# Attention operand loads taken one by one over five tiles, start-up transfers reordered, and pair weights asked for at tick 5

## The chip, the core and the metric

The kernel runs on one core of one Trainium2 chip. The metric is the device time of one execution in microseconds (us). A core has five instruction streams: TensorE (PE, matrix products), VectorE (DVE), ScalarE (ACT), GpSimd (POOL) and SyncE (SP), which here does nothing but issue transfers between DRAM and on-chip memory (DMAs). Each stream runs its instructions in the order in which they were written, and an instruction that must wait holds up everything behind it on the same stream, DMA issues included.

## The reference

One decoder block, on x of 1024 tokens by 1024 channels, all float32:

```
h = rms_norm(x);  z = h @ w_in                    # q, k, v, glu_in, two gates
attention: 3 groups (dilation 1, 4, 16) x 8 heads of 64, window 128 keys,
           relative bias; p = softmax(q k^T / 8 + bias); o = p v
           the 3 groups' outputs are merged by their softmax denominators, @ w_attn_out
conv:      GLU, causal depthwise convolution of 31 taps, layer norm, silu, @ w_conv_out
x = x + rms_norm((sigmoid(z_ga) * attn + sigmoid(z_gc) * conv) @ w_mix_out)
x = x + rms_norm(swiglu(rms_norm(x)))             # hidden width 2816
```

## The kernel before

**Arithmetic.** Every operand of a large product is split into a high part (rounded) and a low part (the rest), and three matmuls of high and low parts make one product. ACT makes the high part, DVE or POOL subtracts it to get the low part. Most products are done in a seven-product block scheme (`winograd`, L320, called for pairs of weight tiles).

**Stages, in PE's order.** `start` (L479) computes the first projections while it loads x and three weight tiles. Then come GLU and gate projections and the query and key projections (`qk_pair`, L778), all by pairs of weight tiles (`pair`, L270), with the convolution on DVE beside them. Then `v` (L891) computes the values, and attention runs beside it: `beat` (L133) steps the generator `attention` (L932) after each matmul at a fixed rate. Attention goes on beside the convolution's output projection (L1444 ff.). Then the mixing projection, the FFN and its output follow.

**Attention.** There are 96 tiles: 12 pairs of heads with 8 query blocks (u = 0 to 7) each. For one tile PE computes scores (`att_s`, L980: matmuls at L995; DVE adds the bias tile and takes the minimum at L998), ACT takes the exponential (`att_e`, L1008), three tiles later PE transposes (`att_t`, L1031) and ACT and DVE split the result (L1036, L1037), and four tiles later PE multiplies with the values (`att_p`, L1052 and L1054) and DVE adds the parts (L1059). The outputs go to DRAM by stores at L1017 and L1021 (`datt`), statistics to `dst`.

**Loads of the next pair.** Queries and keys were stored in DRAM (`dq`, `dk`). `stacks` (L833) issues all loads of one pair of heads: per head a half tile of queries twice (L841, L842, 256 KB each) and the keys (L843, 512 KB), and then the bias tile (L474, 256 KB, from `rep`). `attention` calls it when u has reached 2 (L968). `double` (L849, POOL) copies the queries to the other half of their tiles when u reaches 6 and 7. `values` (L868) loads the next values (`dv`) as soon as the last were split (`value_parts`, L882: ACT L887, POOL L888).

**What sets the order.** Nothing reorders instructions: the order of each stream is that of the program text as it is executed when the kernel is built. `tick` (L115) counts matmul steps and runs steps planned for a tick. `pair` plans the splits of the current weights and the load of the next two tiles (`load_ahead`, L171) at tick `LD` after the pair's start. On-chip tiles come from a pool of 44 buffers of 512 KB (`slot`) and one of 13 buffers of 256 KB (`half`). A new tile takes a released buffer, and the first instruction that writes it waits for the last one that used the buffer, which may be a store that still reads it. SP's DMAs leave in program order, and each waits, besides, for the DMA that was issued eight before it.

Of the kernel before, what the change touches and what calls it, by code (L numbers as in the profile page):

```python
# [10 lines left out]
F32R = mybir.dt.float32r  # L11
# [7 lines left out]
H = 512  # L19
# [13 lines left out]
RV, RU = 0.42, 0.8  # L33


LD, PC = 7, (18, 20, 26)

FIRST = 4

# [17 lines left out]
def f(ap):  # L57
    return ap.bitcast(F32)


class Build:
# [417 lines left out]
    def start(self, jobs):  # L479


        nc = self.nc
        n = len(jobs)
        xs = [self.slot() for _ in range(KT)]
        for i in jobs:
            self.raw[i] = self.slot()
        self.sent = self.queued = jobs[-1] + 1
        for hf in range(2):
            nc.sync.dma_start(xs[0][:, hf * H:(hf + 1) * H], self.xT[0][:, hf * H:(hf + 1) * H])
        self.consts()  # L490
        for i in jobs:
            nc.scalar.dma_start(self.raw[i][:, :256], self.jobs[i][0][:, :256])
        nc.sync.dma_start(xs[1], self.xT[1])
        for i in jobs:
            nc.sync.dma_start(self.raw[i][:, 256:], self.jobs[i][0][:, 256:])
        for kt in range(2, KT):
            nc.sync.dma_start(xs[kt], self.xT[kt])
        self.par = self.small.tile([128, NPAR], F32, name="par")
        nc.gpsimd.dma_start(self.par, self.p_par)
        banks = [[self.bank() for _ in range(2)] for _ in range(n)]  # L500
        W = [(self.slot(F32R), self.slot(F32R)) for _ in range(n)]
        self.hH, self.hL, acc = [], [], None

        def weight_parts(i, kt):
            s = slice(kt * 128, (kt + 2) * 128)
            wh, wl = W[i]
            nc.scalar.copy(wh[:, s], self.raw[jobs[i]][:, s])
            nc.vector.tensor_tensor(wl[:, s], self.raw[jobs[i]][:, s], f(wh[:, s]), op=OP.subtract)

        def square(kt):  # L510
            q = self.slot()
            nc.scalar.activation(q, xs[kt], AF.Square)
            if acc is not None:
                nc.vector.tensor_tensor(q, q, acc, op=OP.add)
            return q

        weight_parts(0, 0)
        for kt in range(KT):
            hi, lo = self.slot(F32R), self.slot(F32R)
            for s in (slice(0, H), slice(H, T)) if kt == 0 else (slice(0, T),):  # L520
                nc.scalar.activation(hi[:, s], xs[kt][:, s], AF.Copy, scale=self.gains[:, kt:kt + 1])
                nc.vector.scalar_tensor_tensor(lo[:, s], xs[kt][:, s], self.gains[:, kt:kt + 1], f(hi[:, s]),
                                               op0=OP.mult, op1=OP.subtract)
            if kt % 2 == 0:
                for i in range(n):
                    if kt or i:
                        weight_parts(i, kt)

            if kt:
                acc = square(kt - 1)  # L530
            self.hH.append(hi)
            self.hL.append(lo)
        acc = square(KT - 1)
        for i in jobs:
            del self.raw[i]
        self.load_ahead(jobs[-1] + 2)
        self.queue_split(jobs[-1] + 2)
        norm = self.rstd(acc, T, self.eps_rms)
        pb = None
        for kt in range(KT):  # L540
            s = slice(kt * 128, (kt + 1) * 128)
            for i in range(n):
                for a, b in ((W[i][0], self.hH), (W[i][0], self.hL), (W[i][1], self.hH)):
                    for hf in range(2):
                        nc.tensor.matmul(banks[i][hf], a[:, s], b[kt][:, hf * H:(hf + 1) * H],  # L545
                                         start=kt == 0 and a is W[i][0] and b is self.hH,
                                         stop=kt == KT - 1 and a is W[i][1])
                self.tick()
            if kt == KT - 3:
                next(norm)  # L550
            if kt == KT - 2:
                try:
                    next(norm)
                except StopIteration as e:
                    pb = e.value
        self.rs = self.slot()
        for hf in range(2):
            nc.scalar.copy(self.rs[:, hf * H:(hf + 1) * H], pb[hf])
        self.xs = xs
        return banks  # L560
# [270 lines left out]


    def stacks(self, g, hp):  # L833

        nc = self.nc
        dk, dq = self.d_qk[g, hp]
        ops = []
        top, low = slice(0, 64), slice(64, 128)
        for h in range(2):
            k, a, b = self.slot(F32R), self.slot(F32R), self.slot(F32R)  # L840
            nc.sync.dma_start(f(a[top]), dq[h][top])  # L841
            nc.sync.dma_start(f(b[low]), dq[h][low])  # L842
            nc.sync.dma_start(f(k), dk[h])  # L843
            ops.append((k, a, b))
        bt = self.bias_tile(g, hp)
        st = self.tiny(96, "stat", 3).rearrange("p (g u e) -> p g u e", g=3, u=8)
        return [g, hp, ops, bt, st]

    def double(self, p, hf):  # L849

# [81 lines left out]
    def attention(self):  # L932

        live, s, total = {}, 0, 96
        order = [(g, 2 * hg + i) for hg in range(2) for g in range(3) for i in range(2)]
        nxt, cur, u, x, V = self.stacks(*order.pop(0)), None, 8, None, None

        def there():
            return nxt[1] // 2 * 3 + nxt[0] < self.vn

        while s < total + self.LP:
            if s < total:
                if x is None and nxt and there():
                    x = self.values(*nxt[:2])
                if u == 8:
                    while not self.normed or x is None:
                        if x is None and there():
                            x = self.values(*nxt[:2])
                        yield 0
                    if cur is None:  # L950
                        self.double(nxt, 0)
                        self.double(nxt, 1)
                    V, cur, u, nxt = [], nxt, 0, None
                live[s] = a = {}
                self.att_s(a, cur, V, u)
                u += 1

                if u in (3, 4):
                    V.append(self.value_parts(x, u - 3))
                    if u == 4:  # L960
                        x = None
                if u == 6 and cur[0] == 2:
                    self.other_stats(cur)
                if u in (6, 7) and nxt:
                    self.double(nxt, u - 6)
                if u == 8:
                    cur[2] = cur[3] = V = None
                if u == 2 and order:  # L968
                    nxt = self.stacks(*order.pop(0))
            if 0 <= s - 1 < total:  # L970
                self.att_e(live[s - 1])
            yield 0
            if 0 <= s - self.LT < total:
                self.att_t(live[s - self.LT])
                yield 0
            if 0 <= s - self.LP < total:
                yield from self.att_p(live.pop(s - self.LP))
            s += 1
# [929 lines left out]
```

## Time and profile before

| what | value |
|---|---|
| time, median of 3 runs (lowest to highest) | 1756.43 us (1753.7 to 1757.82) |
| time of the profiled execution | 1755.95 us |
| span in its trace, first to last instruction | 1754.2 us |
| PE busy | 1713.3 us, 98% of the span |
| DVE, ACT, POOL busy | 1244.9, 794.3, 459.6 us |
| moved by DMA | 277.03 MB, 158 GB/s over the span |
| granted PE clock, mean | 0.992 |

A row of the waits says who waited for whom, the total in us, how many times, and the longest. A row of the timeline has start, duration, engine, line and operation, and in brackets the idle time of the engine just before and what ended it; SPq and ACTq are DMA issues. A row of the windows gives for each engine the busy time in that stretch, then the granted PE clock (1.00 is full), the busy share of the DMA engines and the GB/s moved.

### The profile page before, as it was taken

What the parts mean: (1) busy time and instruction counts of PE and PEld (TensorE: products, weight loads), DVE (VectorE), ACT (ScalarE), POOL (GpSimd) and SP (SyncE); (2) the same over time, 40 slices, a digit from 0 to 9 for tenths busy, and PEclk for the clock granted to TensorE, in tenths of its full rate; (3) what the DMA queues carried; (4) which work ended last, traced back from release to release, by engine and by line L of the source; (5) the groups of instructions that cost most, each with busy time, mean ns of one, the idle gap of its engine ahead of it and who ended that gap; (6) DMA issues with size and microseconds to landing.
All of it is one profiled execution on the core that took longest, in us unless ns stands there. A gap on an engine that the chain in (4) does not pass through costs nothing.

```text
span 1754.2 us, 24483 instructions
## 1 busy us (share of the span) xinstructions
PE 1713.3 (98%) x8698; PEld 1456.1 (83%) x8698; DVE 1244.9 (71%) x2217; ACT 794.3 (45%) x1552; POOL 459.6 (26%) x337
## 2 busy tenths in 40 slices
PE   8999999999999999998899999999999999999998
PEld 6778888887788999998788888888888888888886
DVE  6879988898997666685575665585665655667686
ACT  6344444343344476666543245643333333354453
POOL 0017778787785133342300130000000000000000
PEclk9999999999999999998899999999999999999999
DMA  4342333466678797886755742212232232395234
GB/s 161 122 159 96 124 135 126 151 193 171 165 168 195 234 274 205 226 228 161 202 191 181 279 164 87 96 72 90 91 133 101 91 109 107 132 341 180 96 126 152
DMA packets 186406, 277.03 MB, mean 158 GB/s; under 512 B 56321, under 2 KB 108028, under 8 KB 186284
## 3 DMA queue, kind: packets, MB, share of 16 engines
q1 hardware_dynamic: 185596, 274.84, 49.9%
q8 instruction: 68, 1.11, 0.3%
q14 instruction: 54, 0.44, 0.1%
q10 hardware_dynamic: 576, 0.40, 0.1%
q0 software_dynamic: 112, 0.24, 0.0%
HBM read 184.81 MB, written 95.33 MB: 160 GB/s over the span
## 4 chain that ended last, share of the span: by engine, by line
PE 88%; DMA 3%; ACT 3%; DVE 2%; issue 2%; POOL 1%; SPq 0%; DVEq 0%; ACTq 0%; POOLq 0%
PE p L315 14%; PE p L317 14%; PE p L316 14%; PE p L1792 12%; PE p L303 5%; PE p L299 5%; PE p L301 5%; PE p L1521 5%; PE p L913 2%; PE p L911 2%; PE p L915 2%; PE p L545 2%; PE p L995 2%; PE p L1031 1%; PE p L1054 1%
## 5 line engine op out<-in xcount | busy, mean ns | idle before, releaser
L315 PE MATMUL p<-b,b 128*128 128x512 f32 x1204 | 469.7, 390 | 4.5 <-DVE c L820 2.7
L317 PE MATMUL p<-b,b 128*128 128x512 f32 x1204 | 469.1, 390 | 0.3 <-POOL b L190 0.3
L316 PE MATMUL p<-b,b 128*128 128x512 f32 x1204 | 468.9, 389 | 0.0
L315 PEld LDWEIGHTS p<-b,b 128*128 128x128 f32 x1204 | 226.4, 188 | 53.5 <-DVE c L820 4.1
L317 PEld LDWEIGHTS p<-b,b 128*128 128x128 f32 x1204 | 226.2, 188 | 48.0 <-POOL b L190 1.0
L316 PEld LDWEIGHTS p<-b,b 128*128 128x128 f32 x1204 | 226.4, 188 | 47.3
L189 ACT CAST b<-b 128x1024 fp32r<-128x1024 f32 x131 | 137.8, 1052 | 173.0 <-POOL b L210 65.7
L1792 PE MATMUL p<-b,b 128*128 128x512 f32 x924 | 209.6, 389 | 0.0
L1792 PEld LDWEIGHTS p<-b,b 128*128 128x128 f32 x924 | 173.4, 188 | 36.0
L190 POOL TENSOR_TENSOR b<-b,b 128x1024 fp32r<-128x1024 f32 x66 | 158.9, 2408 | 127.5 <-ACT b L189 109.9
L190 DVE TENSOR_TENSOR b<-b,b 128x1024 fp32r<-128x1024 f32 x65 | 79.5, 1223 | 127.6 <-ACT b L189 127.6
L675 DVE SCALAR_TENSOR_TENSOR p<-b,par,p 128x511 f32<-128x511 f32 (+14 forms) x232 | 163.4, 738 | 0.0
L299 PE MATMUL p<-b,b 128*128 128x512 f32 x368 | 147.9, 402 | 0.0
L303 PE MATMUL p<-b,b 128*128 128x512 f32 x368 | 147.0, 399 | 0.0
L301 PE MATMUL p<-b,b 128*128 128x512 f32 x368 | 146.6, 398 | 0.0
L913 PE MATMUL p<-b,b 128*128 128x256 f32 x384 | 115.7, 301 | 1.5 <-DVE b L183 1.5
L911 PE MATMUL p<-b,b 128*128 128x256 f32 x384 | 115.9, 302 | 0.6 <-ACT b L182 0.6
L915 PE MATMUL p<-b,b 128*128 128x256 f32 x384 | 114.9, 299 | 0.0
L1137 DVE TENSOR_TENSOR b<-b,b 128x512 fp32r<-128x512 f32 x117 | 80.6, 692 | 24.1 <-ACT b L1136 22.4
L1137 DVE TENSOR_TENSOR b<-c,b 128x512 fp32r<-128x512 f32 x101 | 70.1, 694 | 38.1 <-ACT b L1136 37.6
L1136 ACT CAST b<-b 128x512 fp32r<-128x512 f32 x117 | 72.4, 620 | 50.6 <-DVE b L1649 12.6
L1037 DVE TENSOR_TENSOR c<-p,c 128x256 fp32r<-128x256 f32 (+1 forms) x96 | 52.3, 545 | 54.1 <-ACT c L1036 51.8
(224 smaller groups left out, 3020.3 us busy)
## 6 DMA issues: line engine op xcount, KB each, us to landing
b<-w_in SPq DMA_DIRECT2D x53, 512.0 KB, 5.1
b<-w_fi SPq DMA_DIRECT2D x44, 512.0 KB, 5.0
dk<-c SPq DMA_DIRECT2D x96, 128.0 KB, 3.0
dq<-c SPq DMA_DIRECT2D x96, 128.0 KB, 2.4
b<-dq SPq DMA_DIRECT2D x48, 256.0 KB, 7.7
b<-dk SPq DMA_DIRECT2D x24, 512.0 KB, 8.0
dqS<-c SPq DMA_DIRECT2D x44, 256.0 KB, 2.1
b<-w_fo SPq DMA_DIRECT2D x44, 256.0 KB, 4.6
```

Of the source, the lines that this page charges most:

```text
L190: self.wsplit.tensor_tensor(lo, x, f(hi), op=OP.subtract)
L299: nc.tensor.matmul(ps, hi[:, s], a, start=kt == 0, stop=False)
L301: nc.tensor.matmul(ps, hi[:, s], b, start=False, stop=False)
L303: nc.tensor.matmul(ps, lo[:, s], a, start=False, stop=kt == nk - 1)
L315: nc.tensor.matmul(ps, hi[:, s], a, start=first and kt == 0, stop=False, skip_group_check=True)
L316: nc.tensor.matmul(ps, hi[:, s], b, start=False, stop=False, skip_group_check=True)
L317: nc.tensor.matmul(ps, lo[:, s], a, start=False, stop=kt == 3, skip_group_check=True)
L675: nc.vector.scalar_tensor_tensor(A[i][:, j:], src[i][:, :H - j], w[i], A[i][:, j:], op0=OP.mult, op1=OP.add)
L911: nc.tensor.matmul(o, a, hi[:, s], start=kt == 0, stop=False)
L913: nc.tensor.matmul(o, a, lo[:, s], start=False, stop=False)
L1137: nc.vector.tensor_tensor(s[:, 512:512 + n], src, f(s[:, :n]), op=OP.subtract)
L1792: nc.tensor.matmul(acc[t], x, y, start=first and e == 0, stop=last and e == 2, skip_group_check=True)
```

## The change

1. `LD` goes from 7 to 5: the next pair's weights are asked for two ticks sooner.
2. In `start`, the first transfers leave in another order. The left half of the first x tile goes out on ACT's queue ahead of the gains; SP begins with the first quarter of the first weight tile, then the right half of that x tile, the first quarters of the other two weight tiles, the second x tile, the rest of the weights, the rest of x. Before, SP began with both halves of x, and ACT issued the three weight quarters behind the gains.
3. `stacks` only makes the record of the next pair, now when u has reached 1. A new function, `stack_load`, loads one part in each of five tiles: the queries of the first head (u = 1), of the second head (u = 2), the keys of the first (u = 3), of the second (u = 4), the bias tile (u = 5).

```diff
-LD, PC = 7, (18, 20, 26)
+LD, PC = 5, (18, 20, 26)
...
-        for hf in range(2):
-            nc.sync.dma_start(xs[0][:, hf * H:(hf + 1) * H], self.xT[0][:, hf * H:(hf + 1) * H])
+        nc.scalar.dma_start(xs[0][:, :H], self.xT[0][:, :H])
+        w = [(self.raw[i], self.jobs[i][0]) for i in jobs]
+        nc.sync.dma_start(w[0][0][:, :256], w[0][1][:, :256])
+        nc.sync.dma_start(xs[0][:, H:], self.xT[0][:, H:])
         self.consts()
-        for i in jobs:
-            nc.scalar.dma_start(self.raw[i][:, :256], self.jobs[i][0][:, :256])
+        for x, d in w[1:]:
+            nc.sync.dma_start(x[:, :256], d[:, :256])
         nc.sync.dma_start(xs[1], self.xT[1])
-        for i in jobs:
-            nc.sync.dma_start(self.raw[i][:, 256:], self.jobs[i][0][:, 256:])
+        for x, d in w:
+            nc.sync.dma_start(x[:, 256:], d[:, 256:])
...
     def stacks(self, g, hp):
+        st = self.tiny(96, "stat", 3).rearrange("p (g u e) -> p g u e", g=3, u=8)
+        return [g, hp, [[None] * 3, [None] * 3], None, st]
+
+    def stack_load(self, p, i):
...
+        if i < 2:
+            a, b = self.slot(F32R), self.slot(F32R)
+            nc.sync.dma_start(f(a[top]), dq[i][top])
+            nc.sync.dma_start(f(b[low]), dq[i][low])
+            p[2][i][1:] = a, b
+        elif i < 4:
+            k = self.slot(F32R)
+            nc.sync.dma_start(f(k), dk[i - 2])
+            p[2][i - 2][0] = k
+        else:
+            p[3] = self.bias_tile(p[0], p[1])
...
         nxt, cur, u, x, V = self.stacks(*order.pop(0)), None, 8, None, None
+        for i in range(5):
+            self.stack_load(nxt, i)
...
-                if u == 2 and order:
+                if u == 1 and order:
                     nxt = self.stacks(*order.pop(0))
+                if u < 6 and nxt:
+                    self.stack_load(nxt, u - 1)
```

More of the change, by code (lines that the diff above doesn't have):

```diff
@@ L487, in start @@
         self.sent = self.queued = jobs[-1] + 1
-        for hf in range(2):
-            nc.sync.dma_start(xs[0][:, hf * H:(hf + 1) * H], self.xT[0][:, hf * H:(hf + 1) * H])
+        nc.scalar.dma_start(xs[0][:, :H], self.xT[0][:, :H])
+        w = [(self.raw[i], self.jobs[i][0]) for i in jobs]
+        nc.sync.dma_start(w[0][0][:, :256], w[0][1][:, :256])
+        nc.sync.dma_start(xs[0][:, H:], self.xT[0][:, H:])
         self.consts()
-        for i in jobs:
-            nc.scalar.dma_start(self.raw[i][:, :256], self.jobs[i][0][:, :256])
+        for x, d in w[1:]:
+            nc.sync.dma_start(x[:, :256], d[:, :256])
         nc.sync.dma_start(xs[1], self.xT[1])
-        for i in jobs:
-            nc.sync.dma_start(self.raw[i][:, 256:], self.jobs[i][0][:, 256:])
+        for x, d in w:
+            nc.sync.dma_start(x[:, 256:], d[:, 256:])
+        w = x = None
         for kt in range(2, KT):
@@ L833, in stacks @@
     def stacks(self, g, hp):
+        st = self.tiny(96, "stat", 3).rearrange("p (g u e) -> p g u e", g=3, u=8)
+        return [g, hp, [[None] * 3, [None] * 3], None, st]
+    def stack_load(self, p, i):
         nc = self.nc
-        dk, dq = self.d_qk[g, hp]
-        ops = []
+        dk, dq = self.d_qk[p[0], p[1]]
         top, low = slice(0, 64), slice(64, 128)
[L839 to L847, printed above, removed]
+        if i < 2:
[9 more added lines that the diff above has]
+            p[3] = self.bias_tile(p[0], p[1])
     def double(self, p, hf):
```

## The prediction

> **What bounds the kernel now.** I read the page first: one engine is busy nearly all the time.
>
> ```profile
> span 1754.2 us, 24483 instructions
> PE 1713.3 (98%) x8698; PEld 1456.1 (83%) x8698; DVE 1244.9 (71%) x2217; ACT 794.3 (45%) x1552; POOL 459.6 (26%) x337
> ...
> PEclk9999999999999999998899999999999999999999
> ```
>
> PE is the bound. A change that leaves PE's work alone can win only where PE stands still, or where its clock is low: slices 21 and 22 of 40 (about 790 to 877 us), in the attention stage. The second view is PE's waits over the whole span.
>
> ```profile
> PE p L1052 <- issue: 8.5, 1, 8.5
> PE p L545 <- ACT b L521: 6.8, 1, 6.8
> PE p L1052 <- ACT c L1036: 6.2, 1, 6.2
> PE p L315 <- DVE c L820: 2.7, 2, 2.4
> ...
> PE p L315 <- ACT c L329: 1.7, 2, 1.4
> ...
> PE p L317 <- POOL b L190: 0.3, 1, 0.3
> ```
>
> Three waits carry the idle time: the start (6.8) and two single stalls before L1052 (8.5 and 6.2), together 21.5 us. The waits within the two stalls, 809 to 816 and 837 to 847 us, name who is behind them:
>
> ```profile
> ACT b L921 <- DMA dot<-b: 8.0, 1, 8.0
> ...
> PE p L1052 <- ACT c L1036: 6.2, 1, 6.2
> ```
>
> ```profile
> ACT b L887 <- DMA dv<-b: 9.6, 1, 9.6
> DVE c L1037 <- ACT c L1036: 9.6, 1, 9.6
> ...
> PE p L1052 <- issue: 8.5, 1, 8.5
> ```
>
> Neither is a wait for data. L921 and L887 write new tiles into recycled buffers, and stores (of `dot` and `dv`) still read these buffers. ACT runs in order, so the exponentials and splits behind them stand, and PE with them. Why is a store late? SP's timeline shows what was issued just before the `dot` store:
>
> ```profile
> 796.54 0.48 SPq L841 DMA_DIRECT2D b<-dq  x1
> ...
> 799.78 0.63 SPq L843 DMA_DIRECT2D b<-dk  x1
> 801.90 0.38 SPq L474 DMA_DIRECT2D c<-rep  x1
> 803.16 0.32 SPq L1122 DMA_DIRECT2D dot<-b  x1
> ...
> 832.47 0.67 SPq L474 DMA_DIRECT2D c<-rep  x1
> 834.40 1.66 SPq L898 DMA_DIRECT2D dv<-b  x2
> ```
>
> Both stores stand behind one whole burst of `stacks` (2.25 MB). ACT goes on at 813.47 and 844.43, about 10 us after the issues at 803.16 and 834.40:
>
> ```profile
> 813.47 0.59 ACT L921 COPY b<-p 128x512 f32<-128x512 f32 x1 [8.00 <-DMA dot<-b]
> ```
>
> ```profile
> 815.57 0.48 PE L1052 MATMUL p<-b,c 128*128 128x128 f32 x1 [6.18 <-ACT c L1036]
> ```
>
> From ACT's restart to PE's it is 815.57 - 813.47 = 2.1 us. A store of 512 KB without the burst takes 2.9 us to land (`dgc<-b` in the list of DMA issues):
>
> ```profile
> dgc<-b SPq DMA_DIRECT2D x10, 512.0 KB, 2.9
> ```
>
> The last view is the windows around the stalls, for the clock (seventh column) and the GB/s:
>
> ```profile
> 801.60:811.60 10.00, 7.79 (x68) 7.59 (x66) 5.12 (x16) 3.04 (x9) 4.63 (x7) 1.00 1.03 268
> 811.70:821.90 10.20, 6.08 (x27) 5.89 (x28) 3.58 (x13) 4.91 (x17) 1.87 (x4) 0.50 0.50 162
> ...
> 842.40:852.60 10.20, 6.42 (x22) 5.53 (x23) 4.20 (x14) 5.06 (x18) 6.17 (x9) 0.50 0.50 155
> ...
> 439.70:443.00 3.30, 2.95 (x7) 2.37 (x8) 3.30 (x6) 1.29 (x2) 2.53 (x3) 0.50 0.33 66
> ```
>
> After each stall the granted clock is 0.50 for 10.2 us, of which PE works 6.1 and 6.4 us at half speed: 3.0 and 3.2 us lost beside the idle time. The wait of 2.4 us before L315 was followed by 3.3 us at 0.50 as well, and the one of 1.4 us by none.
>
> **The change part by part.** On PE, DVE, POOL and ACT the built program has the same compute instructions in the same order as before; only SP's order, four DMAs of the start and the buffers differ. So nothing is added to PE; all is in waits.
>
> *Loads spread over five tiles, second stall.* In the new order the buffer that L887 takes here is no longer the one that the `dv` stores read. It waits for a subtraction (DVE L183) that ends before ACT comes to it. The first instruction to write the `dv` buffer is now the second head's key load, so this wait moves to SP. The next pair needs those keys five tiles later. The stall goes with its clock: -8.5 - 3.2 = -11.7 us. Late next is SP's queue behind that wait: the values and the bias tile.
>
> *First stall.* L921 still waits for `dot`, but that store now leaves ahead of the second key load and the bias tile, and the first head's queries went out before the statistics store and have landed. That takes 512 + 256 + 512 KB = 1.31 MB out of the queue ahead of it; at the 268 GB/s of the row, 4.9 us. Ends: no stall, if it lands as soon as the 2.9 us store, and all of 6.2. I take 4.9, since the row is of this very stretch: 6.2 - 4.9 = 1.3 us of idle are left. By the 1.4 us wait that costs no clock, so another -3.0: together -7.9 us. Should 2.3 us be left, the 2.4 us row says half clock for 3.3 us: 1.6 us back.
>
> [...]
>
> *The same store before.* DVE waited 2.4 us for the first `dot` store, and PE lost 0.8 us at 788 (its wait for DVE L1037):
>
> ```profile
> 787.07 0.42 DVE L1059 TENSOR_REDUCE b<-p 128x128 f32<-128x256 f32 x1 [2.40 <-DMA dot<-b]
> ```
>
> The store now leaves ahead of the second key load and the bias tile (0.79 MB at 268 GB/s is 2.9 us), and L1059 gets another buffer. -0.8 us.
>
> *What the spreading adds.* The bias tile is asked for when u is 5, four tiles before L998 reads it, and behind the values' load and the `datt` store, which waits for DVE. Before, it was seven tiles ahead. The rows for the time to landing and for the pace:
>
> ```profile
> DMA to landing us min/median/max: 9.7/10.1/10.5
> ```
>
> ```profile
> L998 DVE CUSTOM_DVE_ANT_0 c<-p,c x192: 271/292/426, 626.6 to 896.3; 128x128 f32<-128x128 f32 x104, 128x256 f32<-128x256 f32 x88
> ```
>
> 96 tiles in 269.7 us are 2.8 us each, so four tiles are 11.2 us. The 10.1 us are those of the end of a burst; with the burst gone I expect 4 to 7 us after the issue at most pairs (3 us for an empty queue, 2 to 4 for the values' 512 KB ahead at 218 GB/s). It is near where the queue is full whatever the order, at the first and the last change of pair:
>
> ```profile
> 624.00:646.00 22.00, 21.34 (x180) 20.85 (x179) 13.71 (x50) 16.09 (x49) 7.81 (x10) 1.00 0.93 271
> 646.00:778.00 132.00, 130.18 (x1122) 129.15 (x1121) 94.08 (x329) 86.80 (x286) 49.95 (x62) 1.00 0.80 218
> 862.00:884.00 22.00, 21.12 (x139) 18.43 (x138) 16.05 (x59) 16.31 (x54) 8.57 (x10) 1.00 0.96 304
> ```
>
> There (DMA share 0.93 and 0.96) the same bytes land at the same end, about 645.5 and 882 us, and the bias tile is now last among them; L998 wants it at about 642.8 and 878.5. DVE would be held some 3 us at each. PE has cover: 8.0 us of ACT cost it 6.2, and 9.6 cost it 8.5, so 1.1 to 1.8 us are free, more where it has `v` matmuls to do. I take 1 us each, +2.0 in all; ends 0 and +8 (2 x 2.4 and the clock at each).
>
> *The start.* The first PE instruction waits for ACT, and ACT for the first weight quarter:
>
> ```profile
> 1.24 4.51 DMA b<-w_in
> 5.75 0.02 issue
> ...
> 6.08 0.73 ACT b L521
> ```
>
> It was issued at 1.24 us and is now the first of SP's queue, at 0.75 (where SP's first DMA stood). It also no longer shares the engines with both halves of x ahead of it. Behind it L521 needs the left half of x, as early as before, and the gains, now ACT's second DMA (0.4 us later). The issue alone gives 0.5 us; L521 starts when the last of the three is there. I take 0.8 us; ends 0 and 2.9 (1.24 us, and a clock that is granted a step sooner: PE runs at half speed until 12.7 us). [...]
>
> *Weights two ticks sooner.* SP already waits for the buffer, not for the tick:
>
> ```profile
> SPq L171 <- POOL b L217: 23.5, 11, 4.6
> ```
>
> The new tile's buffer is released by POOL's L217, and SP's order in this stage is unchanged; only at two pairs do buffers change places among instructions released by the same L217. 0 us; ends -0.3 (the only PE wait for POOL L190) and +2.
>
> **The sum**, against the profiled execution's 1755.95 us (span 1754.2): -11.7 - 7.9 - 0.8 + 2.0 - 0.8 = -19.2, so 1736.8. The median of the runs shown is 1756.43, 0.5 above it. I forecast 1737 us.
>
> **The rivals.**
> *The rest of the first stall is longer.* If the queue moves at half the rate I used while the small packets of `dst` pass, `dot` lands 2.4 us later; 3.7 us of idle and 1.6 of clock come back: 1737 + 2.4 + 1.6 = 1741. For it: ACT's wait is still there. Against: the rate is that of the stretch.
> *One long stall stays,* because another recycled buffer is held by a store: 1737 + 11.7 = 1749. For it: the pool hands out buffers in a new order in all of attention, and two such waits fell in by chance. Against: at each buffer that changed hands, the old trace has the release at least 2.4 us before its new writer, most often over 5 us.
> *Nothing measurable:* the queue has the same bytes, and the share of busy DMA is 0.80 from 646 to 778 us; both stalls stay, 1753 to 1760. Against: 837 to 847 us hangs on a single buffer.
> *Slower: the bias tile is late at every change of pair.* If it still takes 10.1 us to land, and is issued 2 us after its tile began (behind `datt` and the values), it comes 0.9 us late at 2.8 us a tile, and 2.5 us late at the 2.4 us that tiles take without stalls. From about 1.5 us of lateness on, PE stands; each of 11 changes then costs PE 1 to 1.5 us, and half clock (1.6 us) where it passes 2: 11 x 3 = 33 us, 1770. For it: it is the load that is issued last and the values are ahead of it. Against: with the burst gone its time to land should be well under 10 us.
>
> **How the numbers follow.** Forecast 0.50 (own range 1731 to 1743), longer rest 0.16, one stall stays 0.13, nothing 0.07, slower 0.14. About 0.2% (3.5 us) is what a measurement of this kernel can tell from no change. Faster: 0.50 + 0.16 + 0.13 = 0.79; same 0.07; slower 0.14. The range leaves out the slower case and most of the no-change case: 1730 (the start's and the first stall's better ends) to 1755.
>
> **What would show it.** Second stall: no ACT wait for `dv<-b`, clock 1.00 in the stretch after it. First stall: ACT's wait for `dot<-b` about 3 us instead of 8.0. Start: first PE matmul near 6.0 us. Bias tile: no DVE L998 wait for `c<-rep` outside the first and the last change of pair. Wrong would be a new PE wait over 3 us between 626 and 900 us, L998 waits on `rep` at most changes, or new waits of the pairs between 120 and 560 us.

## The result and the profile after

The changed kernel takes 1741.24 us (median of 6 runs, 1740.24 to 1743.23) and the kernel before 1755.07 us (6 runs, 1751.55 to 1758.88). The ratio is 0.9923, with a 95% interval of 0.9906 to 0.9941: it is faster by 0.8%, by 13.8 us. The forecast was 1737 us, with 1731 to 1743 as the likeliest case's own range and 1730 to 1755 over the rivals. The sign came out, and of the 19.2 us forecast 13.8 came; the two large terms came out to within 0.2 us, others didn't.

The page of the changed kernel (line numbers are those of the changed file):

```profile
span 1738.5 us, 24500 instructions
PE 1709.7 (98%) x8698; PEld 1453.7 (84%) x8698; DVE 1246.6 (72%) x2217; ACT 794.2 (46%) x1552; POOL 462.3 (27%) x337
...
PEclk9999999999999999999999999999999999999999
```

The two slices with an 8 in the clock row (the 19th and 20th of the 40, not the 21st and 22nd; the times given for them are right) are gone. PE's waits over the whole span:

```profile
PE p L548 <- ACT b L524: 6.6, 1, 6.6
PE p L1064 <- ACT c L1048: 5.1, 2, 4.3
PE p L315 <- DVE c L823: 2.8, 2, 2.5
```

The stall of 8.5 us has no successor at its place, and the one of 6.2 us has left 0.8 us. But there is a wait of 4.3 us that no row of before showed. Both traces hold the same 8698 matmuls in the same order, so the k-th of the one can be set against the k-th of the other, and the span cut into stretches at the same work (us in the two profiled executions):

| stretch, by matmul number | before, where | before | after | difference |
|---|---|---|---|---|
| start, to 30 | 0 to 17 | 16.73 | 16.43 | -0.30 |
| pairs, 30 to 2600 | 17 to 587 | 569.79 | 569.04 | -0.75 |
| attention to 3850 | 587 to 736 | 149.12 | 149.41 | +0.29 |
| 3850 to 4440 | 736 to 808 | 71.98 | 69.78 | -2.20 |
| **first stall**, 4440 to 4590 | 808 to 837 | 28.94 | 20.94 | -8.00 |
| **second stall**, 4590 to 4640 | 837 to 856 | 19.31 | 7.46 | -11.85 |
| **new stall**, 4640 to 4680 | 856 to 862 | 5.79 | 13.85 | +8.06 |
| 4680 to 4830 | 862 to 885 | 23.71 | 22.76 | -0.95 |
| rest | 885 to 1747 | 861.79 | 861.81 | +0.02 |

The two stalls were worth what the forecast said, and 8.1 us of it went into a stall right behind them. The first stall, by ACT's waits from 800 to 812 us of the changed kernel:

```profile
ACT b L929 <- DMA dot<-b: 2.6, 1, 2.6
```

L929 is the old L921; it waited 8.0 us. The new stall, by ACT's and PE's waits from 825 to 842 us, and the clock behind it:

```profile
ACT b L1148 <- DMA datt<-b: 6.7, 1, 6.7
```

```profile
PE p L1064 <- ACT c L1048: 4.3, 1, 4.3
```

```profile
838.60:845.40 6.80, 6.55 (x24) 5.79 (x25) 3.64 (x14) 3.20 (x12) 0.00 (x0) 0.50 0.62 145
```

Again ACT waits for a store to have read a buffer (L1148, the old L1136, makes the first half of a split for the output projection). SP's timeline says why `datt` left late:

```profile
813.51 1.51 SPq L1033 DMA_DIRECT2D dst<-stat  x2
...
818.29 4.41 SPq L906 DMA_DIRECT2D dv<-b  x2
822.79 1.01 SPq L852 DMA_DIRECT2D b<-dk  x1
823.92 0.41 SPq L1218 DMA_DIRECT2D c<-dact  x1
830.05 0.32 SPq L852 DMA_DIRECT2D b<-dk  x1
830.79 1.91 SPq L1033 DMA_DIRECT2D datt<-b  x2
```

and SP's own waits from 812 to 842 us name what it stood for at 824 to 830:

```profile
SPq L852 <- DMA dv<-b: 5.7, 1, 5.7
```

The second key load took over the buffer of the `dv` store, as forecast, and SP stood for it. Behind it in program order is the `datt` store. The wait had only gone from ACT to SP, and came back to ACT through a second store. And the `dv` store itself, issued from 818.29 on, let SP go on only at 830. The windows show what the queue did then:

```profile
816.00:822.00 6.00, 6.00 (x44) 5.43 (x43) 4.21 (x15) 5.33 (x16) 1.28 (x1) 1.00 0.40 18
822.00:830.00 8.00, 8.00 (x57) 7.24 (x56) 6.35 (x21) 5.34 (x18) 4.01 (x6) 1.00 1.02 284
```

For six microseconds 18 GB/s were moved with loads of `dact`, weights and queries on their way, right behind two `dst` stores. The experiments had to tell three things apart: the buffer, SP's stand, and this slow stretch.

### The profile page after: what moved, and what is told of

The parts are those of the page before. It is cut to its first block, busy times and chain, and to the rows that moved or that the text cites. A ratio compares the mean times of both kernels' runs of the same rounds, so it can differ in the third digit from the quotient of the medians.

```text
span 1738.5 us, 24500 instructions
## 1 busy us (share of the span) xinstructions
PE 1709.7 (98%) x8698; PEld 1453.7 (84%) x8698; DVE 1246.6 (72%) x2217; ACT 794.2 (46%) x1552; POOL 462.3 (27%) x337
## 2 busy tenths in 40 slices
DMA packets 186406, 277.03 MB, mean 159 GB/s; under 512 B 56321, under 2 KB 108028, under 8 KB 186284
## 4 chain that ended last, share of the span: by engine, by line
PE 88%; DMA 3%; ACT 3%; DVE 2%; issue 2%; POOL 1%; SPq 1%; DVEq 0%; ACTq 0%; POOLq 0%
PE p L315 14%; PE p L316 14%; PE p L317 14%; PE p L1804 12%; PE p L1533 5%; PE p L299 5%; PE p L303 5%; PE p L301 5%; PE p L921 2%; PE p L919 2%; PE p L923 2%; PE p L548 2%; PE p L1007 2%; PE p L1043 1%; PE p L1066 1%
## 5 line engine op out<-in xcount | busy, mean ns | idle before, releaser
L315 PE MATMUL p<-b,b 128*128 128x512 f32 x1204 | 469.7, 390 | 4.2 <-DVE c L823 2.8
L317 PE MATMUL p<-b,b 128*128 128x512 f32 x1204 | 469.4, 390 | 0.0
L316 PE MATMUL p<-b,b 128*128 128x512 f32 x1204 | 469.0, 390 | 0.0
L315 PEld LDWEIGHTS p<-b,b 128*128 128x128 f32 x1204 | 226.4, 188 | 53.3 <-DVE c L823 4.0
L1804 PE MATMUL p<-b,b 128*128 128x512 f32 x924 | 209.6, 389 | 0.0
L299 PE MATMUL p<-b,b 128*128 128x512 f32 x368 | 147.9, 402 | 0.0
L303 PE MATMUL p<-b,b 128*128 128x512 f32 x368 | 146.8, 399 | 0.0
L301 PE MATMUL p<-b,b 128*128 128x512 f32 x368 | 146.5, 398 | 0.0
L921 PE MATMUL p<-b,b 128*128 128x256 f32 x384 | 115.1, 300 | 1.5 <-DVE b L183 1.5
L1148 ACT CAST b<-b 128x512 fp32r<-128x512 f32 x117 | 72.4, 619 | 50.0 <-DVE b L381 13.1
L1533 PE MATMUL p<-b,b 128*128 128x512 f32 x384 | 88.9, 391 | 0.0
```

The source lines that it names most:

```text
L299: nc.tensor.matmul(ps, hi[:, s], a, start=kt == 0, stop=False)
L301: nc.tensor.matmul(ps, hi[:, s], b, start=False, stop=False)
L303: nc.tensor.matmul(ps, lo[:, s], a, start=False, stop=kt == nk - 1)
L315: nc.tensor.matmul(ps, hi[:, s], a, start=first and kt == 0, stop=False, skip_group_check=True)
L316: nc.tensor.matmul(ps, hi[:, s], b, start=False, stop=False, skip_group_check=True)
L317: nc.tensor.matmul(ps, lo[:, s], a, start=False, stop=kt == 3, skip_group_check=True)
```

## The experiments

Each time stands beside runs of the kernel before on the same chip. These took 1755.07 us beside the change, 1753.15 beside only_spread, before_hold, after_hold and datt_first, 1751.35 beside before_hold2, after_hold2, datt_hold and stat_act, and 1751.55 beside the other four. So rows are compared by their ratios; their medians can be set against each other, and against a forecast of theirs, only to about 4 us. Since the times of one kernel spread by several us as well (see the last section), the stretch from matmul 4440 to 4830, which holds all three stalls, is the sharper measure; before it is 77.75 us and after 65.01. It comes from one trace each, and the clock moves it too: after and only_spread differ by 3.8 us with the same loads in attention (mean granted clock 0.996 and 0.994).

| kernel | median us | ratio to before | 95% interval | 4440 to 4590 | to 4640 | to 4680 | to 4830 | sum |
|---|---|---|---|---|---|---|---|---|
| before | 1755.07 | | | 28.94 | 19.31 | 5.79 | 23.71 | 77.75 |
| after | 1741.24 | 0.9923 | 0.9906 to 0.9941 | 20.94 | 7.46 | 13.85 | 22.76 | 65.01 |
| only_spread | 1739.62 | 0.9930 | 0.9907 to 0.9953 | 24.52 | 7.46 | 14.33 | 22.48 | 68.79 |
| before_hold | 1737.89 | 0.9925 | 0.9903 to 0.9947 | 22.12 | 12.11 | 7.54 | 24.18 | 65.95 |
| before_hold2 | 1743.16 | 0.9946 | 0.9925 to 0.9967 | 23.96 | 14.50 | 7.02 | 22.28 | 67.76 |
| after_hold | 1742.91 | 0.9951 | 0.9933 to 0.9969 | 24.66 | 8.73 | 9.35 | 25.73 | 68.47 |
| after_hold2 | 1738.33 | 0.9913 | 0.9886 to 0.9940 | 21.77 | 7.44 | 12.24 | 23.64 | 65.09 |
| datt_first | 1735.18 | 0.9908 | 0.9888 to 0.9929 | 19.27 | 7.46 | 7.41 | 29.86 | 64.00 |
| datt_hold | 1734.66 | 0.9894 | 0.9860 to 0.9928 | 19.27 | 7.45 | 9.18 | 25.99 | 61.89 |
| stat_act | 1737.25 | 0.9905 | 0.9878 to 0.9932 | 19.27 | 7.46 | 13.62 | 22.15 | 62.50 |
| bias_late | 1740.35 | 0.9934 | 0.9918 to 0.9951 | 24.40 | 7.46 | 14.31 | 22.15 | 68.32 |
| bias_key | 1735.48 | 0.9908 | 0.9895 to 0.9922 | 19.27 | 7.46 | 11.27 | 23.26 | 61.26 |
| bias_key_act | 1735.65 | 0.9904 | 0.9887 to 0.9921 | 19.27 | 7.46 | 7.56 | 28.29 | 62.58 |
| stat_rows | 1727.98 | 0.9864 | 0.9850 to 0.9878 | 19.92 | 7.45 | 5.81 | 22.14 | 55.32 |

**only_spread**: part 3 of the change alone.

```diff
-LD, PC = 5, (18, 20, 26)
+LD, PC = 7, (18, 20, 26)
 # and start() as before
```

> The kernel before with the spread loads alone (start and weights' tick as before). Theory: the two stalls of attention are what the change moves, and the new stall of 4.3 us before L1064 at 834 us comes from the spreading too; start and weights are worth about 1 us: 1742 us, first matmul at 6.85 us as before. Rival: the start and the weights' tick carry a good part (the matmuls stand 1.3 us earlier by 432 us, and 1 us of that could multiply later): 1745 us or more.

It is as fast as the whole change, and the new stall is there (PE's wait before L1061, L1064's counterpart, is 4.1 us). So, to within these intervals, the gain and the new stall are the spreading's.

**before_hold** and **before_hold2**: is it the buffers alone? The pool gives a buffer away after the last recorded use of its tile; a late copy of one column is such a use.

```diff
 # before.py
+    def touch(self, x):
+        self.nc.gpsimd.tensor_copy(self.tiny(1, "touch", 1), x[:, :1])   # before_hold2: vector
...
+            self.later(10, lambda x=x: self.touch(x))                    # before_hold2: 7
             self.vn += i == 6
...
             self.nc.sync.dma_start(self.d_ot[hp], hi)
+            self.later(10, lambda hi=hi: self.touch(hi))
```

> The kernel before, its burst of loads kept; the buffers that the dv and dot stores read are kept from the pool for 10 ticks more by a POOL copy of one column that reads them. Theory (the stalls are waits for two recycled buffers, not for data): no ACT wait for dot or dv over 1 us, neither of the two PE waits of 6.2 and 8.5 us, clock 1.00 throughout 800 to 850 us: 1755 less 11.7 and 9.2 = 1734 us (1730 to 1738), no worse than the change itself. Rival (the burst as such keeps the queue full, and what else stands behind it, values, datt, the bias tile, is late in its turn): one or both stalls come back under another name, 1745 to 1755 us.

> The kernel before with its burst, the buffers of the dv and dot stores kept from the pool by a DVE copy of one column, 7 ticks later (in before_hold POOL made this copy, and stood 5.9 us itself ahead of it, which cost PE 2.8 us and a half clock). Theory (two recycled buffers were the whole of the stalls): no PE wait over 1.3 us between 790 and 850 us, 1737.9 less 2.8 and 1.7 = 1733 us (1730 to 1736), better than the change. Rival (the burst makes datt and the values late, as ACT's wait of 6.9 us for datt in before_hold hints): a stall of 2 us or more stays, 1737 to 1742 us.

Both old stalls go without any spreading, so they were waits for those two buffers. What before_hold keeps is the price of its own POOL copy, which PE felt at 2.8 us and, behind it, 3.4 us of half clock; in the same trace ACT stands 6.9 us for `datt`. But before_hold2, which should have been free of that, shows the rival. Its waits from 825 to 845 us:

```profile
DVE b L1063 <- DMA datt<-b: 7.3, 1, 7.3
...
PE p L1056 <- DVE b L1063: 4.2, 1, 4.2
```

With the `dv` buffer out of the pool, the next tile got `datt`'s. That store stands behind the same burst, so the stall had another name. The theory that two buffers were the whole of it falls: a buffer only says who waits, while late stores say that somebody will.

**after_hold** and **after_hold2**: the same copies in the changed kernel, so that SP needn't stand for the `dv` store (after_hold2: DVE, 4 ticks, the `dv` tiles only).

> The changed kernel with the same POOL copies, so that the second key load finds another buffer than the one that the dv store reads. Theory (SP stands 5.7 us before that key load, and the datt store behind it holds ACT's L1148 and so PE): datt is issued at about 826 us instead of 830.8 and lands at 831 to 833 instead of 835.8; PE's wait of 4.3 us falls to 1.5 or less and the half clock of 6.8 us goes: 1741 less 3 to 4 less 3.4 = 1734 us (1731 to 1736). Rival (the queue is jammed by itself between 816 and 822 us, when it moves next to nothing behind the small packets of dst): datt lands no earlier than 835 us and the time stays at 1740 to 1742 us.

> The changed kernel with a DVE copy of one column that keeps the dv buffer from the pool 4 ticks longer; after_hold had POOL copies, which stood 3.8 us and held L933. Theory (SP's stand before the second key load is what makes datt late): SP's stand is gone, ACT's wait for datt falls from 6.7 to 4.8 us or less, PE's wait from 4.3 to about 1.1 us, no half clock at 838 us: 1741.2 less 3.2 and 3.4 = 1734.6 us (1732 to 1737). Rival (the queue alone): PE's wait stays above 3 us, 1740 to 1742 us.

In after_hold the new stall fell from 4.3 to 1.1 us, but POOL's copies stood 3.8 us themselves and cost more than that elsewhere. In after_hold2 SP no longer stands before the key load, `datt` leaves at 826.72 instead of 830.79, and ACT still waits:

```profile
ACT b L1152 <- DMA datt<-b: 4.6, 1, 4.6
```

PE's longest wait there halves to 2.2 us, but the clock was at half for 10.2 us behind it (mean granted clock 0.995 over the span, 0.996 in the changed kernel), and nothing was won. About half of PE's 4.3 us goes with SP's stand; the other half doesn't. The slow stretch is in this trace too: 31 GB/s from 816 to 822 us.

**datt_first**, **datt_hold**, **bias_key**: the order behind SP's stand.

```diff
 # datt_first (after.py); datt_hold adds the DVE copy of after_hold2
-                if u < 6 and nxt:
+                if u < 6 and u != 4 and nxt:
                     self.stack_load(nxt, u - 1)
...
                 yield from self.att_p(live.pop(s - self.LP))
+            if u == 4 and nxt:
+                self.stack_load(nxt, 3)
 # bias_key: "if u < 4 and nxt" above, and here stack_load(nxt, 4), then stack_load(nxt, 3)
```

> The changed kernel with the second key load issued behind the datt store instead of ahead of it; the key load still takes the buffer of the dv store. Theory (what counts is that datt stands behind a waiting load on SP): SP still stands for the dv store, but datt is out already: PE's wait at 834 us 1.5 us or less, full clock: 1734 to 1736 us. Rival (datt is late because of the queue): 1739 to 1742 us. If the key load itself then comes late, PE would wait before the scores of the next pair instead (a wait for b<-dk): 1741 us or more.

> Both: the second key load behind the datt store, and the dv buffer kept from the pool by the DVE copy. Theory (in datt_first the bias tile stood behind the key load that waited for the dv store, hence DVE's wait of 3.9 us and PE's of 3.5 at 854 us): neither stall, full clock from 443 us to the end: 1735.2 less 3.5 and 3.5 = 1728 us (1726 to 1732). Rival (the bias tile is late at this place whatever stands ahead of it on SP, since the queue is full): PE's wait before L1009 stays above 2 us, 1733 to 1736 us.

> The changed kernel with the last two loads turned round and put behind the datt store: datt, bias tile, second key load. The key load still takes the dv store's buffer and SP still stands for it, but datt and the bias tile are out by then. Theory: neither the stall at 834 us (4.3 us and 3.4 us of half clock) nor datt_first's at 854 us (3.5 us and half clock): 1735.2 less 7.1 = 1728 us (1725 to 1732). Rival (what stands behind the key load now, the values, becomes late): a PE wait for b<-dv or value parts, 1734 us or more.

With `datt` ahead of the key load, the stall at 834 us is gone in datt_first (stretch to 4680: 7.41 us). A pair later the bias tile is late; its waits from 840 to 862 us:

```profile
DVE c L1012 <- DMA c<-rep: 3.9, 1, 3.9
...
PE p L1009 <- issue: 3.5, 1, 3.5
```

In datt_hold, where SP doesn't stand, this is 2.0 us instead of 3.5. In bias_key the bias tile is in time, and a PE wait of 1.4 us at 831 us and one of 0.9 us at 857 stay. Each order moves the lateness on: datt_first's median lies in the range expected of it, but with another stall in place of the one removed, and neither of the others came to its 1728 us. In all three the stretch is shorter than the change's 65.01 us, but their intervals overlap with the change's: none is shown to be faster than it by its time.

**stat_act** and **bias_key_act**: the `dst` stores from ACT's queue.

```diff
-            self.nc.sync.dma_start(d, src)
+            (q or self.nc.sync).dma_start(d, src)      # q = self.nc.scalar for dst
```

> The changed kernel with the dst stores (8 KB in packets of 16 bytes) issued from ACT's queue instead of SP's. Between 816 and 822 us the changed kernel moves 18 GB/s with seven loads under way, just behind two dst stores. Theory (the small packets stop what stands behind them in the same queue): the stretch moves over 150 GB/s, the dv store lands some 4 us sooner, SP's stand before the key load falls from 5.7 to below 2 us and PE's wait from 4.3 to 1 us: 1735 us (1732 to 1738). Rival (the packets hold up the DMA engines themselves, whichever queue they come from): the stretch stays below 50 GB/s and the time at 1740 to 1743 us.

> bias_key with the dst stores on ACT's queue as in stat_act, where the rest of the first stall (0.8 and 0.4 us) went to nothing. Theory: 1 us below bias_key, within its interval. Rival (ACT, which has to issue 18 more DMAs of 0.5 us, is late for the splits): equal or 2 us above.

The slow stretch stays, only earlier. It is in stat_act's windows:

```profile
813.00:818.00 5.00, 5.00 (x38) 4.55 (x37) 4.12 (x14) 4.66 (x14) 1.19 (x1) 1.00 0.29 20
818.00:822.00 4.00, 4.00 (x29) 3.61 (x28) 3.01 (x11) 3.39 (x10) 1.15 (x2) 1.00 0.90 242
```

SP stands 6.0 us before the key load, and PE's wait is 3.9 us. The median lies in the theory's range, but none of its signs is there: by mechanism the rival is right. The rest of the first stall is gone (19.27 us in the first column), as in datt_first and bias_key, where `dst` stayed on SP; the new stall is not. What holds up the loads is not that `dst` is ahead of them in SP's queue: with `dst` on ACT's queue 20 GB/s were moved from 813 to 818 us, against the changed kernel's 18 GB/s from 816 to 822. bias_key_act, with 12 more DMAs on ACT's queue (not 18), was no better than bias_key: there PE waits 3.1 us at 853 us, before the scores whose second key tile came last.

**stat_rows**: the same bytes of `dst` in fewer pieces.

```diff
-            self.tokens_out(g, self.d_st[g, a["hp"]], st[:, g])
+            d = self.d_st[g, a["hp"]].rearrange("(p u) e -> p u e", u=8)
+            for b in range(g + 1):
+                s = slice(b * 4, 8 if g == 0 else b * 4 + 4)
+                self.nc.sync.dma_start(d[:, s], st[:, g, s])
```

> The changed kernel with the dst stores written as rows (one piece of 64 or 128 bytes for each partition, 128 pieces a store) instead of 512 to 1024 pieces of 16 bytes. The statistics of groups 0 and 1 then lie in DRAM in another order of tokens, so the merged outputs are other numbers; the work is the same. Theory (the many small pieces stop all DMA engines: in stat_act the stretch behind them stood at 7 GB/s too, from another queue): no stretch below 100 GB/s at 814 to 822 us, the dv store lands 4 us sooner, SP's stand before the second key load is 2 us or less, PE's wait of 4.3 us falls to 1 or less: 1741.2 less 3.5 and 3.4 = 1734 us (1731 to 1737). Rival (the stretch is slow for another reason, the loads of queries themselves or what they wait for): below 50 GB/s still, 1739 to 1742 us.

The queue now runs through. Its windows, the same stretch of work:

```profile
814.00:818.00 4.00, 4.00 (x30) 3.63 (x29) 3.80 (x11) 3.99 (x13) 0.58 (x1) 1.00 0.81 262
818.00:822.00 4.00, 4.00 (x30) 3.62 (x29) 3.12 (x11) 3.11 (x9) 1.49 (x2) 1.00 1.06 327
```

against these of the changed kernel:

```profile
814.00:818.00 4.00, 4.00 (x33) 3.80 (x32) 2.22 (x8) 2.35 (x8) 0.00 (x0) 1.00 0.63 131
818.00:822.00 4.00, 4.00 (x30) 3.63 (x29) 2.92 (x14) 3.43 (x12) 1.28 (x1) 1.00 0.48 21
```

ACT's waits for stores from 780 to 875 us shrink to

```profile
ACT b L929 <- DMA dot<-b: 1.6, 1, 1.6
ACT b L1151 <- DMA datt<-b: 1.3, 1, 1.3
```

and no PE wait of attention is over 0.8 us; the granted clock is 1.00 in every window from 800 to 836 us and 0.999 over the span. The order of SP is that of the changed kernel, the second key load's wait for the `dv` store is still there (3.0 us instead of 5.7), and it costs nothing. 1728 us is the lowest time of all, 6 us below what the theory asked for, of which 3.5 us are those by which the kernel before was faster beside it. Its interval lies clear of the change's: 0.9864 against 0.9923 are some 10 us, and the stretch is 9.7 us shorter. The page counts 49665 packets under 512 bytes instead of 56321: 6656 pieces fewer, out of 277 MB that are the same.

So in the changed kernel the root of the new stall was the time that stores and loads took behind `dst`'s small pieces. For the two stalls of the kernel before the same is likely but not shown: the store that came late had a slow stretch behind a `dst` store ahead of it in both (47 GB/s from 796 to 798 us, 27 from 826 to 830), but no run wrote `dst` in rows with the old loads. The pieces themselves are soon through: in the changed kernel the 1024 of them between 814 and 818 us took 9 to 10 ns each on the DMA engines. What stands is what comes next: the 37 packets of 2 KB between 818 and 822 us took 0.8 us each on average, against 0.085 us at the median of the trace's 2 KB packets.

This kernel leaves out putting the statistics back in the order of tokens, so its merged outputs are other numbers. A kernel for use would have to sort them at another place, and none such was tried.

**bias_late**: the price of the forecast's slower rival.

```diff
-                if u < 6 and nxt:
+                if u < 5 and nxt:
                     self.stack_load(nxt, u - 1)
+                if u == 6 and nxt:
+                    self.stack_load(nxt, 4)
```

> The changed kernel with the bias tile asked for when u is 6 instead of 5, three tiles before it is read instead of four. It prices the case of the forecast in which the bias tile is late at every change of pair. By the forecast's prices: it lands 6.8 us after its issue at the median and 9.2 at most, three tiles are 8.4 us less some 2 us to the issue: late by up to 3 us at half of the 11 changes, each 1 us of PE and half clock at one or two: 1741 and 5 to 10 more, 1746 to 1751 us. Rival (PE has v matmuls in hand wherever DVE stands): 1743 us or less, with DVE waits for rep but no PE wait over 1 us.

Nothing is lost, though the tile is asked for 2.8 us later at every change of pair:

```profile
DVE c L1012 <- DMA c<-rep: 2.7, 3, 1.1
```

Three short waits of DVE in 11 changes, and no wait of PE for them. So the case in which the bias tile is late at every change doesn't come about even with a tile less of room, since the tile lands 6.8 us after its issue and not 10.1. The price of 3 us for a change at which it is late by 1.5 us or more was not put to the test.

## Why the prediction was right, and where not

The two stalls and what held them were read rightly; the wait that the change moved to SP was priced at nothing, and there a new stall came. The prediction had named a new PE wait over 3 us between 626 and 900 us as a sign of being wrong, and the one of 4.3 us at 834 us is that.

- **Second stall, -11.7**: -11.85. The mechanism held, the buffer's wait did move to SP's key load.
- **"Late next is SP's queue behind that wait: the values and the bias tile."** This step failed. What was late next was the `datt` store, for which ACT's L1148 waits. The same wait is in the kernel before, hidden behind the longer stall: there the second `datt` store landed at 849.60 us, and ACT came to its L1136 only at 850.95. So no row showed it, and its buffer was none of those that changed hands. The stretch grew by 8.06 us: 4.3 us of idle time, and some 3.3 for the 6.55 us that PE worked at half clock.
- **First stall, -7.9**: -8.0. ACT's wait fell from 8.0 to 2.6 us, and 0.8 us of PE's is left (forecast 1.3), with full clock. Here that was luck too: in only_spread a PE wait of 1.2 us at the same place had a half clock behind it (stretch 24.52 instead of 20.94).
- **Bias tile, +2.0**: nothing. DVE waited 1.5 and 1.7 us at the first and the last change of pair, where the forecast put it, and PE didn't feel it. It landed 6.8 us after its issue at the median, within the 4 to 7 expected.
- **L1059 and the store before, -0.8**: -1.0 at that place (matmuls 4270 to 4440); another 1.2 us from 736 to 788 us and 0.95 us behind the stalls were not in the sum.
- **Start, -0.8**: about -0.2. In the kernels with the old start the first matmul began at 6.85, 6.47, 7.16 and 6.96 us, in ten with the new one at 6.28 to 6.89, with a mean of 6.68. The 0.5 us of the earlier issue alone was nearer than 0.8, and still too much. What came late were the `gains` (rows below).
- **Weights two ticks sooner, 0**: 0. Matmuls 400 to 1850 of the pairs take 330.39 us with either value in every other trace (the profile of before has 330.99).
- **The sum**: -23.7 without the new stall, -15.7 with it in the two traces, -19.2 forecast. The forecast is nearer to the measured time than its terms are, since time that it didn't count as saved, and prices that weren't paid, stand against the stall that it didn't see: that is luck.
- **The rivals**: "longer rest of the first stall" gave the measured 1741, and its premise, a queue that is slow while `dst`'s small packets pass, is the one that stat_rows bears out; but it looked for the delay at `dot`, and it fell on `dv` and `datt`. "One long stall stays" was the nearest in kind, with the wrong place and price. The argument against it, that each buffer which changed hands is released at least 2.4 us before its new writer, didn't hold for the `dv` buffer: in the changed kernel SP stood 5.7 us for its release.

The start's rows, first the kernel before and then the changed one:

```profile
5.77 0.41 ACT L507 CAST b<-b 128x256 fp32r<-128x256 f32 x1 [3.10 <-DMA b<-w_in]
```

```profile
4.65 0.41 ACT L510 CAST b<-b 128x256 fp32r<-128x256 f32 x1 [1.48 <-DMA b<-w_in]
5.83 1.33 ACT L524 ACTIVATE b<-b,gains 128x512 fp32r<-128x512 f32 x2 [0.78 <-DMA gains<-p_par]
```

The first weight quarter came 1.1 us sooner, as the forecast wanted, and then ACT waited for the `gains`, which were issued 0.4 us later, as the forecast had it, but landed 0.95 us later (5.75 us instead of 4.80).

That the changed order itself caused the lateness behind the new stall is only half true: SP's stand of 5.7 us is the change's, the slow stretch behind `dst` is in the kernel before as well (27 GB/s from 826 to 830 us):

```profile
826.00:830.00 4.00, 4.00 (x30) 3.72 (x30) 2.84 (x12) 2.95 (x9) 0.00 (x0) 1.00 0.21 27
```

Why so few small pieces stop all else for 4 to 6 us, the runs don't show: the pieces' number was changed, and their length with it.

## What to carry to other kernels

Where an engine waits for a store to release a buffer, look first at why the store is late, and for the slowest stretch of the queue ahead of it; here another buffer or another order only changed who waited. When a wait moves to an engine that issues DMAs, list every DMA behind it in program order, and for each store who needs its buffer next, also where the profile shows no wait because a longer one covers it. And two transfers of 8 KB in 16-byte pieces took the place of some 1.7 MB of loads here (an estimate: 6 us of a queue that then ran at 284 GB/s).

## What the runs showed that was not expected

**The clock's fall does not follow from the length of the wait alone.** The forecast took 1.4 us of waiting to be free and 2.4 us to cost 3.3 us of half clock. The wait before L315 (L318 in before_hold) at about 436 us is 2.4 us in before_hold and 2.5 us in the changed kernel; behind it, in before_hold and then in the changed kernel, stands

```profile
439.00:443.00 4.00, 4.00 (x19) 3.29 (x19) 4.00 (x6) 1.79 (x3) 2.76 (x3) 1.00 0.48 90
```

```profile
439.30:442.60 3.30, 3.30 (x9) 2.59 (x8) 3.30 (x4) 1.01 (x2) 2.22 (x2) 0.50 0.40 79
```

full clock in the one, half in the other. In bias_late waits of 1.1 and 0.4 us at 805 us (PE is busy for 1.29 of 2.80 us) were followed by 6.7 us at half:

```profile
805.00:807.80 2.80, 1.29 (x10) 0.95 (x9) 1.22 (x3) 2.58 (x11) 0.97 (x2) 1.00 1.07 293
808.00:814.70 6.70, 6.70 (x34) 6.70 (x33) 3.28 (x11) 2.93 (x10) 0.00 (x0) 0.50 0.24 75
```

Between the start and the end, the granted clock was at half for 3.4, 10.2 and 10.2 us in the kernel before, and for 3.4 and 6.8 us in the changed kernel. So the forecast's prices, worked out from the lengths of two waits, are not enough: 1.5 us in two pieces was followed by half clock, as was 2.5 us in one and the 2.4 us before L315 in the kernel before, while 2.4 us in before_hold wasn't. What else the fall depends on, the runs don't show.

**The same program starts at two speeds.** Between 9.7 and 12.9 us PE did 15 matmuls in only_spread and 9 in before, with the same start code:

```profile
9.70:12.90 3.20, 3.20 (x15) 2.63 (x14) 1.61 (x2) 2.36 (x3) 0.00 (x0) 1.00 1.04 412
```

```profile
9.70:12.90 3.20, 3.20 (x9) 2.46 (x8) 1.71 (x2) 2.60 (x4) 0.00 (x0) 1.00 1.03 410
```

The clock's column says nothing in these two rows: the trace's record of the clock begins only at full clock, at 9.61 us in only_spread and 12.96 us in before, and that PE ran at half speed ahead of this is read from the number of matmuls, 9 in the 3.2 us against 15. From the first matmul to the thirtieth the traces take 8.5 to 10.0 us, and around the wait at 436 us (matmuls 1850 to 1890) 10.8 to 13.8 us, whatever the kernel, while matmuls 5200 to the last take 787.9 us in all. So a good part of the spread of one kernel's times, 1751.55 to 1758.88 us before, is likely due to when the clock is granted (an estimate from these two stretches, which differ by up to 1.5 and 3.0 us between the traces; not shown, as only one run of each kernel has a trace), and a difference of 3 us between two kernels is better read from the stretch that was changed.
